# A causal mask in stick-breaking attention: from a TensorE product to a predicated copy and a select

## The chip, the cores and the metric

The kernel runs on one core of one Trainium2 chip. The metric is the device time of one launch in microseconds (us); the median of several executions is compared. Times inside an execution come from a profiled one and count from the start of its span.

## What is computed

The reference is a small decoder trunk of two layers on 1024 positions and a model width of 1024. Layer 0 mixes positions with sliding-window attention, layer 1 with stick-breaking attention; each is followed by a SwiGLU block. The change touches layer 1's mixer alone, whose core is, for each of 16 heads of 64 and each block of 128 queries:

```python
z = jnp.einsum('bqhd,bshd->bhqs', qb, k).astype(jnp.float32) * scale
strict = k_idx < t_idx
log_beta = jax.nn.log_sigmoid(z)
log_one_minus = jnp.where(strict, jax.nn.log_sigmoid(-z), 0.0)
rc = lax.cumsum(log_one_minus, axis=3, reverse=True)
after = jnp.pad(rc[..., 1:], ((0, 0), (0, 0), (0, 0), (0, 1)))
a = jnp.where(strict, jnp.exp(log_beta + after), 0.0)
o = jnp.einsum('bhqs,bshd->bqhd', a.astype(v.dtype), v)
```

The kernel works with the sigmoids themselves: a reversed running product of sigmoid(-z) stands for the exponential of the reversed sum. Where a key is not strictly before its query, the first sigmoid has to count as 1 and the second as 0.

## The kernel before

All of the kernel is one function, `build` (line 65), with nested helpers; `mm` (L107) and `tr` (L115) issue products and transposes, so every one of these has L108 or L116 in the profile, and `sub` (L118) issues a subtraction with L119. Layer 1's mixer works on **eight pairs of heads** (`p` = 0 to 7). For each pair there are three streams of work:

- `proj_gen` (L1026) makes the pair's queries, keys and values from the normalised input: products into the PSUM banks `psd`, then copies to `QK` and `V` with a high part (ScalarE) and a rest (`sub` on DVE). It first loads the pair's weights with `load_b` (L981), whose split into a high part `whl` (ScalarE, L308) and a rest runs on POOL (L309) for two of the three weights of a pair.
- `scores` (L1076) takes one head of the pair (`par`) and two blocks `i` = 2c and 2c+1 of 128 queries against the `L` = 128(i+1) keys up to the end of the block. One or two pieces of at most 512 keys each get two products into a bank `psz` (high and rest of the keys). On the last piece a third product with the bf16 matrices `identb` and `maskb` adds -1e30 where a key is not strictly before the query (L1093). ScalarE then makes `nb` = sigmoid(-z) (L1094) and `bb` = sigmoid(z) (L1095). When the block is whole, DVE runs the reversed running product over `nb` in place (L1101, one scan of L elements) and POOL multiplies `bb` by it (L1103). The result waits in the list `ready`.
- `values` (L1110) runs two steps of the order behind: it transposes `bb` on TensorE into `pst` (L116), splits the transposed tile into `ah` (ScalarE, L1124) and `al` (`sub` on DVE, L119) and multiplies both by `V` into `psa`.

For pairs 0 to 6 `weave` (L1152) interleaves the steps of `scores`, `values` and `proj_gen` of the next pair, for c = 3, 2, 0, 1 with the first head and then the same with the second: the query blocks come as 6, 7, 4, 5, 0, 1, 2, 3, twice in a pair. In these pairs TensorE's order is fixed by hand: `chained` (L99) makes each product follow the one before. The order on the other engines is set by the planner of the framework from the dependencies and the order of the program; each engine then works its queue strictly in that order. The eighth pair has no projection beside it; its scores and values run one after the other, with the split of the output weights (`load_o`, L363 to L369) on DVE and ScalarE between them.

Buffers: `nb` has 3, `bb` 6, `psz` 3 banks, `ah` and `al` 2 each. The constants `identb` and `maskb` are made once at the start (L126 to L135). `up`, a mask of ones above the diagonal that layer 0 uses, is made at L173 to L175 in the same manner as the new `upd`.

Of the kernel before, what the change touches and what calls it, by code (L numbers as in the profile page):

```python
# [9 lines left out]
BF16 = mybir.dt.bfloat16  # L10
I32 = mybir.dt.int32
U32 = mybir.dt.uint32
AF = mybir.ActivationFunctionType
ALU = mybir.AluOpType
# [4 lines left out]
P = 128  # L19
# [7 lines left out]
NEG = -1.0e30  # L27
# [37 lines left out]
def build(tc, x_in, c_in, pos_in, ada_w, ada_b, n1g, n2g, wqkv_a, qn_a, kn_a, sinks, wo_a,  # L65
          wqkv_b, wo_b, w_gate, w_up, w_down, out):
    nc = tc.nc
# [5 lines left out]
    cons = ctx.enter_context(tc.tile_pool(name="cons", bufs=1, side="left"))  # L73
# [8 lines left out]
    def nm(s):  # L82
        uid[0] += 1
        return f"{s}_{uid[0]}"

    def bank(tag, dt=F32):
        return ps.tile([P, 512], dt, tag=tag, name=nm("ps" + tag), bufs=BUFS[tag])
# [11 lines left out]
    def chained(i):  # L99

        if pe["on"] and pe["prev"] is not None:
            tc.add_manual_dep(i.ins, pe["prev"].name,
                              mybir.DependencyInfo(mybir.DependencyClass.NoSync, mybir.DependencyReason.DATA),
                              reason="order")
        pe["prev"] = i.ins if pe["on"] else None

    def mm(o, l, r, start, stop, more=False):  # L107
        chained(nc.tensor.matmul(o, l, r, start=start, stop=stop, skip_group_check=more))  # L108
# [13 lines left out]
    ident = cons.tile([P, P], F32, name="ident")  # L122
    make_identity(nc, ident)
    identr = cons.tile([P, P], F32R, name="identr")
    nc.vector.tensor_copy(identr, ident)
    identb = cons.tile([P, P], BF16, name="identb")  # L126
    nc.vector.tensor_copy(identb, ident)
    ones = cons.tile([P, P], F32, name="ones")
    nc.vector.memset(ones, 1.0)
    mhalf = cons.tile([P, 8], F32, name="mhalf")  # L130
    nc.vector.memset(mhalf, -0.5)

    maskb = cons.tile([P, P], BF16, name="maskb")
    nc.gpsimd.memset(maskb, 0.0)
    nc.gpsimd.affine_select(maskb, maskb, [[-1, P]], ALU.is_gt, NEG, base=0, channel_multiplier=1)  # L135
    negt = cons.tile([P, 1], F32, name="negt")
    nc.vector.memset(negt, NEG)
    up = cons.tile([P, P], U32, name="up")


    cols = cons.tile([P, 32], F32, name="cols")
# [31 lines left out]
    upf = st.tile([P, P], F32, name="upf")  # L173
    nc.gpsimd.affine_select(upf, ones, [[1, P]], ALU.is_gt, 0.0, base=0, channel_multiplier=-1)
    nc.vector.tensor_copy(up, upf)  # L175
    r1 = st.tile([32, P], F32, name="r1")
    r2 = st.tile([96, P], F32, name="r2")
    r3 = st.tile([NB, P], I32, name="r3")
# [897 lines left out]
    def scores(p, par, c, Q, K, kl, V):  # L1076

        bs = []
        for i in (2 * c, 2 * c + 1):
            L = P * (i + 1)  # L1080
            n = max(256, L if L <= 512 else L // 2)
            nb = wb.tile([P, S], F32, tag="nb", name=nm("nb"), bufs=3)
            bb = wb.tile([P, S], F32, tag="bb", name=nm("bb"), bufs=6)
            tq = slice(i * P, i * P + P)
            for s0 in range(0, L, n):
                pz = bank("z")
                o = pz[:, 0:n]
                last = s0 + n >= L
                mm(o, Q[par][:, tq], K[par][:, s0 : s0 + n], True, False)
                mm(o, Q[par][:, tq], kl[par][:, s0 : s0 + n], False, not last)  # L1090
                e = min(n, L - s0)
                if last:
                    mm(pz[:, e - P : e], identb, maskb, False, True)  # L1093
                nc.scalar.activation(nb[:, s0 : s0 + e], pz[:, 0:e], AF.Sigmoid, scale=-1.0)  # L1094
                nc.scalar.activation(bb[:, s0 : s0 + e], pz[:, 0:e], AF.Sigmoid)  # L1095
                if not last:
                    yield
            if i == 2 * c:
                nc.gpsimd.memset(bb[:, L : L + P], 0.0)
            rv = nb[:, 0:L][:, ::-1]  # L1100
            nc.vector.tensor_tensor_scan(rv, rv, ones[:, 0:1].to_broadcast([P, L]), initial=1.0,  # L1101
                                         op0=ALU.mult, op1=ALU.mult)
            nc.gpsimd.tensor_tensor(bb[:, 0 : L - 1], bb[:, 0 : L - 1], nb[:, 1:L], op=ALU.mult)  # L1103
            bs.append(bb)
            if i == 2 * c:
                yield
        ready.append((p, par, c, V, bs))
        yield
# [59 lines left out]
    for p in range(8):  # L1168
        cur = nxt
        if p < 7:  # L1170
            pe["on"], pe["prev"] = True, None
            if p == 6:
                for _ in range(4):
                    xq.tile([P, S], F32R, tag="xq", name=nm("QK"), bufs=NQ)
            gen = proj_gen(p + 1)
            nxt = next(gen)
            for n, (par, c) in enumerate((par, c) for par in range(2) for c in (3, 2, 0, 1)):
                parts = [(scores(p, par, c, *cur), STOPS[c])]
                if len(ready) >= LAG:
                    v = ready.pop(0)  # L1180
                    parts.append((values(*v), 2 * v[2] + 2))
                parts.append((gen, (7, 6, 6, 6)[n % 4]))
                weave(parts)
            drain(gen)
            pe["on"] = False
        else:
            W = wo_tiles(hp_) + wo_tiles(hp_)
            for n, (c, par) in enumerate((c, par) for c in range(4) for par in range(2)):
                drain(scores(p, par, c, *cur))
                while len(ready) > (1 if n < 7 else 0):  # L1190
                    drain(values(*ready.pop(0)))
                load_o(W, wo_b[0], n, row_b, ad, "ad")
# [39 lines left out]
```

## Time and profile before

| quantity | value |
|---|---|
| median of three runs | 2514.96 us (2512.82 to 2516.09) |
| the profiled execution's own time | 2506.01 us |
| its span | 2504.3 us |
| TensorE products busy | 2359.5 us, 94% |
| DVE busy | 1604.8 us, 64% |
| ScalarE (ACT) busy | 1036.6 us, 41% |
| GpSimd (POOL) busy | 646.4 us, 26% |

Stick-breaking attention takes the stretch from about 1199 to 1710 us of the span. In the rows below PE is TensorE, PEld its loading of weights, DVE VectorE, ACT ScalarE and POOL GpSimd. A timeline row gives the start, the duration, the engine, the line, the operation, the tile written and the tiles read, the shapes and how many instructions are merged; what stands in brackets is how long the engine had been idle before and what ended that. Products overlap on TensorE, so that their pace is read from starts and not from durations. A duration includes the time in which an instruction that has started cannot go on.

### The profile page before, as it was taken

How to read it: one execution, taken by the hardware profiler on the slowest of the kernel's cores; microseconds unless marked ns; L12 is line 12 of the kernel's file. 1: busy time of each engine (PE TensorE's matmuls, PEld its weight loads, DVE VectorE, ACT ScalarE, POOL GpSimd, SP SyncE). 2: the span in 40 equal slices, each digit the busy share in tenths (PEclk: the TensorE clock that was granted, in tenths of full speed). 3: DMA queues.
4: the chain of work that ended last, by engine and by line, in shares of the span. 5: the costliest groups of instructions: out<-in, count | busy, mean ns of one | idle time of the engine just before them, and what ended most of it. 6: DMA issues, size and time to landing. Idle time of an engine off the chain costs nothing.

```text
span 2504.3 us, 31440 instructions
## 1 busy us (share of the span) xinstructions
PE 2359.5 (94%) x11404; PEld 1934.1 (77%) x11404; DVE 1604.8 (64%) x2319; ACT 1036.6 (41%) x2029; POOL 646.4 (26%) x671
## 2 busy tenths in 40 slices
PE   6899899799999999999999999988979999999999
PEld 5677677578787878887788888777758888887887
DVE  7679955765767677536677676696375454557553
ACT  4487723423232332104666666573343333323110
POOL 2344512223232300001444444341212322310000
PEclk9799899899999999999999999999989999999999
DMA  8113398143536264203222222127522222227211
GB/s 288 51 50 120 110 228 249 62 130 122 175 120 182 95 238 143 82 9 101 70 58 60 60 56 53 41 80 168 143 76 74 82 93 68 91 86 257 84 51 68
DMA packets 187195, 273.78 MB, mean 109 GB/s; under 512 B 11792, under 2 KB 131744, under 8 KB 187040
## 3 DMA queue, kind: packets, MB, share of 16 engines
q1 hardware_dynamic: 186416, 271.63, 35.2%
q8 instruction: 90, 1.47, 0.2%
q14 instruction: 65, 0.53, 0.1%
q10 hardware_dynamic: 624, 0.14, 0.0%
HBM read 206.72 MB, written 56.62 MB: 105 GB/s over the span
## 4 chain that ended last, share of the span: by engine, by line
PE 70%; DVE 9%; DMA 4%; issue 2%; ACT 2%; POOL 1%; SPq 0%; DVEq 0%; ACTq 0%; POOLq 0%
PE psz L108 24%; PE psd L108 21%; PE pst L108 16%; PE psa L108 5%; DMA ada<-in_ada_w_dram 2%; PE pst L116 2%; DVE nb L1101 2%; DVE acc L268 1%; DVE al L119 1%; DVE lT L119 1%; DVE Wl L309 0%; DMA wr<-in_wo_b_dram 0%; DVE QK L119 0%; DVE sl L631 0%; ACT nb L1094 0%
## 5 line engine op out<-in xcount | busy, mean ns | idle before, releaser
L630 ACT CAST sh<-rg 128x512 fp32r<-128x512 f32 x308 | 191.5, 622 | 565.6 <-PE psz L108 246.1
L631 DVE TENSOR_TENSOR sl<-rg,sh 128x512 fp32r<-128x512 f32 x308 | 244.8, 795 | 94.0 <-ACT sh L630 94.0
L108 PE MATMUL psd<-hth,whl 128*128 128x512 f32 x768 | 304.3, 415 | 0.1
L1103 POOL TENSOR_TENSOR bb<-bb,nb 128x895 f32<-128x895 f32 (+7 forms) x128 | 179.1, 1402 | 248.7 <-DVE nb L1101 159.5
L1101 DVE TENSOR_TENSOR_SCAN nb<-nb,ones 128x896 f32<-128x896 f32 (+7 forms) x128 | 192.4, 1508 | 44.3 <-ACT nb L1094 41.9
L308 ACT CAST dh<-raw 128x1024 fp32r<-128x1024 f32 x88 | 87.9, 1048 | 277.8 <-PE psa L108 174.9
L803 POOL TENSOR_TENSOR rg<-rg,rg 128x512 f32<-128x512 f32 x44 | 58.3, 1324 | 459.8 <-DMA rg<-in_w_up_dram 361.0
L108 PEld LDWEIGHTS psd<-hth,whl 128*128 128x128 f32 x768 | 146.5, 191 | 22.2 <-issue 1.3
L108 PE MATMUL psz<-hT,sh 128*128 128x512 f32 x352 | 139.5, 399 | 19.0 <-ACT hT L684 10.8
L108 PE MATMUL psd<-htl,whl 128*128 128x512 f32 x384 | 152.3, 399 | 1.8 <-DVE htl L119 1.6
L119 DVE TENSOR_TENSOR al<-pst,ah 128x512 fp32r<-128x512 f32 x160 | 108.3, 684 | 62.1 <-ACT ah L1124 59.5
L108 PE MATMUL psz<-lT,sh 128*128 128x512 f32 x352 | 140.0, 398 | 2.7 <-DVE lT L119 2.7
L108 PE MATMUL psz<-hT,sl 128*128 128x512 f32 x352 | 139.0, 395 | 0.0
L108 PE MATMUL psd<-hB,sl 128*128 128x512 f32 x352 | 137.4, 390 | 0.0
L108 PE MATMUL psd<-hB,sh 128*128 128x512 f32 x352 | 137.3, 390 | 0.0
L108 PE MATMUL psd<-lB,sh 128*128 128x512 f32 x352 | 137.0, 389 | 0.0
L268 DVE SCALAR_TENSOR_TENSOR acc<-ada,condT,acc 128x1024 f32<-128x1024 f32 x77 | 111.0, 1441 | 25.5 <-DMA ada<-in_ada_w_dram 24.8
L1094 ACT ACTIVATE nb<-psz 128x448 f32<-128x448 f32 (+3 forms) x192 | 95.3, 496 | 65.6 <-PE psz L108 61.3
L1124 ACT CAST ah<-pst 128x512 fp32r<-128x512 f32 x160 | 94.2, 591 | 54.1 <-PE pst L116 51.8
L309 DVE TENSOR_TENSOR dl<-raw,dh 128x1024 fp32r<-128x1024 f32 x88 | 104.6, 1220 | 9.8 <-ACT dh L308 9.8
L108 PE MATMUL psz<-QK,QK 128*128 128x384 f32 (+4 forms) x384 | 104.7, 356 | 2.5 <-ACT bb L1095 2.4
L108 PE MATMUL psa<-al,V 128*128 128x256 f32 x320 | 88.9, 299 | 17.5 <-DVE al L119 16.7
(325 smaller groups left out, 6336.8 us busy)
## 6 DMA issues: line engine op xcount, KB each, us to landing
ada<-in_ada_w_dram SPq DMA_DIRECT2D x96, 512.0 KB, 4.6
rg<-in_w_gate_dram SPq DMA_DIRECT2D x44, 512.0 KB, 3.6
rg<-in_w_up_dram SPq DMA_DIRECT2D x44, 512.0 KB, 5.7
raw<-hid SPq DMA_DIRECT2D x44, 512.0 KB, 6.6
raw<-in_w_down_dram SPq DMA_DIRECT2D x44, 512.0 KB, 4.4
hid<-f SPq DMA_DIRECT2D x64, 256.0 KB, 2.1
wr<-in_wqkv_b_dram SPq DMA_DIRECT2D x24, 512.0 KB, 4.2
odA<-ob SPq DMA_DIRECT2D x32, 256.0 KB, 2.5
```

The costliest lines, as they stand in the source:

```text
L108: chained(nc.tensor.matmul(o, l, r, start=start, stop=stop, skip_group_check=more))
L119: return nc.vector.tensor_tensor(o, a, h.bitcast(F32), op=ALU.subtract)
L268: i = nc.vector.scalar_tensor_tensor(a, wt, condT[:, j : j + 1], a, op0=ALU.mult, op1=ALU.add)
L308: nc.scalar.copy(h, raw)
L309: (eng or nc.vector).tensor_tensor(l, raw, h.bitcast(F32), op=ALU.subtract)
L630: nc.scalar.copy(hv, src)
L631: nc.vector.tensor_tensor(lv, src, hv.bitcast(F32), op=ALU.subtract)
L803: nc.gpsimd.tensor_tensor(A[1, 0], A[1, 0], A[1, 1], op=ALU.add)
L1094: nc.scalar.activation(nb[:, s0 : s0 + e], pz[:, 0:e], AF.Sigmoid, scale=-1.0)
L1101: nc.vector.tensor_tensor_scan(rv, rv, ones[:, 0:1].to_broadcast([P, L]), initial=1.0, op0=ALU.mult, op1=ALU.mult)
L1103: nc.gpsimd.tensor_tensor(bb[:, 0 : L - 1], bb[:, 0 : L - 1], nb[:, 1:L], op=ALU.mult)
L1124: nc.scalar.copy(ah_, pt)
```

## The change

The mask product is left out, and with it its two constants. The sigmoids of the last 128 keys of a block are masked instead after ScalarE has made them: DVE copies ones over `nb` where a new mask `upd` (made once, on POOL and DVE) is not zero, in front of the scan, and POOL replaces `bb` by zero where the key is not strictly before the query, in front of its multiplication.

```diff
-    identb = cons.tile([P, P], BF16, name="identb")
-    nc.vector.tensor_copy(identb, ident)
...
-    maskb = cons.tile([P, P], BF16, name="maskb")
-    nc.gpsimd.memset(maskb, 0.0)
-    nc.gpsimd.affine_select(maskb, maskb, [[-1, P]], ALU.is_gt, NEG, base=0, channel_multiplier=1)
...
+    upd = cons.tile([P, P], U32, name="upd")
...
+    nc.gpsimd.affine_select(upf, ones, [[1, P]], ALU.is_ge, 0.0, base=0, channel_multiplier=-1)
+    nc.vector.tensor_copy(upd, upf)
...
                 mm(o, Q[par][:, tq], K[par][:, s0 : s0 + n], True, False)
-                mm(o, Q[par][:, tq], kl[par][:, s0 : s0 + n], False, not last)
+                mm(o, Q[par][:, tq], kl[par][:, s0 : s0 + n], False, True)
                 e = min(n, L - s0)
-                if last:
-                    mm(pz[:, e - P : e], identb, maskb, False, True)
                 nc.scalar.activation(nb[:, s0 : s0 + e], pz[:, 0:e], AF.Sigmoid, scale=-1.0)
                 nc.scalar.activation(bb[:, s0 : s0 + e], pz[:, 0:e], AF.Sigmoid)
                 if not last:
                     yield
+            nc.vector.copy_predicated(nb[:, L - P : L], upd, ones)
+            nc.gpsimd.affine_select(bb[:, L - P : L], bb[:, L - P : L], [[-1, P]], ALU.is_gt, 0.0, base=0, channel_multiplier=1)
             if i == 2 * c:
                 nc.gpsimd.memset(bb[:, L : L + P], 0.0)
             rv = nb[:, 0:L][:, ::-1]
```

## Rows read from the trace of the kernel before

**Rows 1.** The page: the chain that ended last, by engine.

```profile
PE 70%; DVE 9%; DMA 4%; issue 2%; ACT 2%; POOL 1%; SPq 0%; DVEq 0%; ACTq 0%; POOLq 0%
```

**Rows 2.** Busy time per stretch: length; PE, PEld, DVE, ACT, POOL; clock; DMA.

```profile
1380.00:1440.00 60.00, 59.40 (x350) 49.39 (x349) 42.75 (x46) 41.50 (x88) 27.98 (x24) 1.00 0.23 62
1660.00:1705.00 45.00, 32.18 (x173) 26.40 (x171) 45.00 (x37) 32.37 (x69) 24.66 (x20) 0.84 0.29 76
```

**Rows 3.** Timeline of TensorE, two score pieces of 448 keys, the second with the mask product.

```profile
1451.72 0.57 PE L108 MATMUL psz<-QK,QK 128*128 128x448 f32 x2
...
1452.36 0.40 PE L108 MATMUL psd<-htl,whl 128*128 128x512 f32 x1
...
1453.96 0.57 PE L108 MATMUL psz<-QK,QK 128*128 128x448 f32 x2
...
1454.73 0.39 PE L108 MATMUL psd<-htl,whl 128*128 128x512 f32 x1
```

**Rows 4.** Timeline of TensorE, the products that wait for `al`, two halves.

```profile
1465.88 0.39 PE L108 MATMUL psa<-al,V 128*128 128x256 f32 x1 [0.48 <-DVE al L119]
...
1498.05 0.38 PE L108 MATMUL psa<-al,V 128*128 128x256 f32 x1
```

**Rows 5.** Timeline of DVE, half of a pair that ends at 1498.

```profile
1487.84 2.02 DVE L1101 TENSOR_TENSOR_SCAN nb<-nb,ones 128x896 f32<-128x896 f32 x1 [0.51 <-ACT nb L1094]
1491.50 2.42 DVE L1101 TENSOR_TENSOR_SCAN nb<-nb,ones 128x1024 f32<-128x1024 f32 x1 [1.64 <-ACT nb L1094]
1493.85 1.38 DVE L119 TENSOR_TENSOR QK<-psd,QK 64x512 fp32r<-64x512 f32 x2
...
1495.87 1.55 DVE L1101 TENSOR_TENSOR_SCAN nb<-nb,ones 128x640 f32<-128x640 f32 x1
```

**Rows 6.** Timeline of ACT, the same half, the last piece of block 7's `bb`.

```profile
1491.30 0.59 ACT L1095 ACTIVATE bb<-psz 128x512 f32<-128x512 f32 x1
```

**Rows 7.** Timeline of POOL, the same half.

```profile
1490.01 1.77 POOL L1103 TENSOR_TENSOR bb<-bb,nb 128x895 f32<-128x895 f32 x1 [3.81 <-ACT ob L1145]
1494.07 2.00 POOL L1103 TENSOR_TENSOR bb<-bb,nb 128x1023 f32<-128x1023 f32 x1 [2.29 <-PE psz L108]
1496.04 3.57 POOL L309 TENSOR_TENSOR whl<-wr,whl 128x1024 fp32r<-128x1024 f32 x1
```

**Rows 8.** One line's instructions on POOL: L309, ns minimum/median/maximum, first and last start.

```profile
L309 POOL TENSOR_TENSOR whl<-wr,whl x14: 2347/2399/3574, 1188.0 to 1586.2; 128x1024 fp32r<-128x1024 f32 x14
```

**Rows 9.** Timeline of DVE, half of a pair that ends at 1466.

```profile
1458.96 2.42 DVE L1101 TENSOR_TENSOR_SCAN nb<-nb,ones 128x1024 f32<-128x1024 f32 x1 [1.64 <-ACT nb L1094]
...
1463.61 1.49 DVE L1101 TENSOR_TENSOR_SCAN nb<-nb,ones 128x640 f32<-128x640 f32 x1
1465.13 0.69 DVE L119 TENSOR_TENSOR al<-pst,ah 128x512 fp32r<-128x512 f32 x1
```

**Rows 10.** Timeline of DVE, last pair.

```profile
1674.29 1.19 DVE L309 TENSOR_TENSOR Wl<-wr,Wh 128x1024 fp32r<-128x1024 f32 x1
1675.40 2.87 DVE L1101 TENSOR_TENSOR_SCAN nb<-nb,ones 128x768 f32<-128x768 f32 x1
...
1688.94 3.56 DVE L1101 TENSOR_TENSOR_SCAN nb<-nb,ones 128x1024 f32<-128x1024 f32 x1
```

**Rows 11.** Timeline of POOL, last pair, and one multiplication from a half before.

```profile
1465.25 1.32 POOL L1103 TENSOR_TENSOR bb<-bb,nb 128x639 f32<-128x639 f32 x1 [1.58 <-DVE nb L1101]
...
1674.51 2.15 POOL L1103 TENSOR_TENSOR bb<-bb,nb 128x639 f32<-128x639 f32 x1 [3.92 <-DVE nb L1101]
...
1688.58 1.77 POOL L1103 TENSOR_TENSOR bb<-bb,nb 128x895 f32<-128x895 f32 x1 [1.49 <-ACT bb L1095]
```

**Rows 12.** Groups by line: DVE's predicated copy of layer 0, DVE's `V` rests.

```profile
L524 DVE COPY_PREDICATED sm<-up,psz 128x256 f32<-128x256 uint32 x56 | 23.1, 439 | 5.2 <-ACT sm L520 4.7
...
L119 DVE TENSOR_TENSOR V<-pst,V 128x256 fp32r<-128x256 f32 x21 | 8.9, 425 | 16.8 <-ACT V L1073 16.7
```

**Rows 13.** One line's instructions: POOL's select for `up`, at the kernel's start.

```profile
L174 POOL TENSOR_SCALAR_AFFINE_SELECT upf<-ones x1: 294/294/294, 1.7 to 1.7; 128x128 f32<-128x128 f32 x1
```

## The prediction

> **What bounds the kernel now.** I read the chain that ended last, then the busy time by stretch, then the timelines of one pair of heads. The chain is TensorE for 70% of the span, DVE for 9% [rows 1], so a product that goes is worth something only where TensorE does not wait, and DVE matters in places. The stretches show two different stages [rows 2]: in the woven pairs 0 to 6 TensorE is busy 59.4 of 60 us at a granted clock of 1.00 (2.4 GHz), in the last pair DVE is busy 45.0 of 45 us, TensorE only 32.2. The timelines of a pair show that even the first stage is not TensorE's alone. Once in each half of a pair (one head's eight blocks) TensorE stops at a product that needs `al`: 0.48 us idle ahead of 1465.88, and a stop too short to be marked ahead of 1498.05 [rows 4]. DVE is what is late: from the scan of block 7 on it has no pause worth the name: scan of 1024, rests of `QK`, an `al`, scan of 640, `al` [rows 5, 9]. So a half has two parts: some 8 us from block 7's scores to that `al`, set by DVE and by POOL beside it, and some 24 us set by TensorE.
>
> **What is removed.** One mask product per block: 16 in a pair, 112 in pairs 0 to 6, 16 in the last. Its price is read by comparing two pieces of 448 keys in the same company, one with and one without it [rows 3]: from the first score product to the second projection product after it, 1451.72 to 1452.36 is 0.64 us, 1453.96 to 1454.73 is 0.77. So 0.13 us each. Of a half's eight, those of blocks 7, 4 and 5 lie ahead of the wait and only lengthen it when they go; five count: 0.65 us a half. ScalarE can start block 7's sigmoids some 0.1 us earlier, which I carry below. In the last pair TensorE waits anyway: nothing.
>
> The Trainium skill, "TensorE: Matmul & The Clock Gate", section "Back-to-back issue gap", gives some 81 ns for a product of 128 columns in a stream with loads. By it 112 products would be an estimated 9.1 us and not 14.6; the trace's 0.13 us is the measurement of this stream and decides.
>
> **What is added.** The copy: 128 columns of f32, which the trace does not show. Layer 0's is 256 wide at 0.439 us [rows 12]. DVE's subtractions of 256 and 512 columns take 0.425 and 0.69 [rows 9, 12], 1.04 ns a column, so half the width is 0.13 less: 0.30 us. Bounds: 0.22 (as wide a share as half of 0.439) and 0.44. The select of 128 x 128 stands in the trace at 0.294 us [rows 13]. The edits at the start exchange a POOL select and a DVE copy for the like, 1.2 ms ahead of this stage: nothing.
>
> Behind the waiting copy stand the scan and then `QK`, `al`, for which TensorE waits. Behind the waiting select stand POOL's multiplication of the same block and the split L309.
>
> **Who may run beside whom.** DVE's scan and POOL's multiplication do not run side by side. At 1688.58 POOL starts 1.77 us of multiplication; the scan of 1024 that starts at 1688.94 takes 3.56 instead of 2.42 [rows 10, 11, 5]. And when two such DVE instructions follow each other, a POOL instruction that is waiting gets in between: at 1674.29 DVE subtracts until 1675.48; POOL's multiplication, started at 1674.51, takes 2.15 instead of 1.32, so it ran from about 1675.3 to 1676.66; the scan queued right behind DVE's subtraction, 1675.40, takes 2.87 and so had to let it pass [rows 10, 11]. In the before a scan is one instruction and POOL waits behind it. The change puts a second one ahead of it, and with it a gap.
>
> The Trainium skill, "SBUF — State Buffer", section "Who interferes with whom", states that DVE with two SBUF inputs and GpSimd reading SBUF exclude each other for a whole instruction. The rows agree for scan and multiplication; no row shows it for the select or the copy. By that rule both take part, each new POOL read included, which speaks against the change. In my sum the select's block has the bounds 0 and 0.29 us; I take 0.29 where it arrives between copy and scan, since the multiplication's row is the nearest.
>
> **A half with the split L309 in it** [rows 5 to 7]. Block 6: copy 0.30, scan to about 1490.1; the select, whose `bb` comes while the scan runs, waits for its end and takes until 1490.4; POOL's multiplication then ends at 1492.2 instead of 1491.78. Block 7: `nb` ready at 1491.3; the copy waits for POOL until 1492.2 and ends at 1492.5; the select, ready since 1491.9, goes next, to 1492.8; the scan (2.42 less 0.13 of waiting) ends at 1495.1 instead of 1493.92. `QK` and an `al`, 1.38 and 0.69 [rows 9], take 2.1: 1497.2. POOL multiplies from 1495.1 to 1497.1 and then has L309, 2.40 us when alone [rows 8]; it took 3.57 because the scan of block 4 was ahead of it. Now the copy arrives when L309 has started, or goes first and lets L309 in before the scan: 1499.5 either way. Copy, select and scan, 0.30 + 0.29 + 1.49, and `al`, 0.69: 1502.3, where TensorE went on at 1498.05 [rows 4]. The wait grows by 4.3 us.
>
> **A half without it** [rows 9]. The scan of block 7 ends 1.2 later, at 1462.6; `al` and `QK` (2.2 from scan to scan) bring 1464.8; POOL has just ended its multiplication, and select and copy, 0.6, make it 1465.3; scan and `al` 1467.5 against 1465.8: some 1.6 us more.
>
> **The sum.** The 3.57 us form of L309 stands in six of the 14 halves (the timeline has it every 64.4 us); in the last of them TensorE soon waits for a weight load anyway, so I count five. 5 x (4.3 - 0.65) = 18.3; 9 x (1.6 - 0.65) = 8.6. In the last pair DVE has no idle time [rows 2], so 16 copies add 16 x 0.30 = 4.8; its selects I leave at nothing, with 16 x 0.29 = 4.7 as the other bound. Together +31.7 us. The rows are of an execution of 2506.0 us, 9 us below the median of 2515.0; the difference is put on the median: **2546 us**.
>
> **Rivals.**
> - *No long block.* L309 comes at another place of POOL's queue (the planner may move it), all else as above: 14 x 0.95 = 13.3, plus 4.8: 2533. For it: POOL's queue gets 16 more instructions a pair. Against: L309 has no tie to the selects and stood between blocks 7 and 4 every time.
> - *Only the copies count.* Select and copy do not exclude the other engine, or do so unnoticed: two copies a half, 0.60, less 0.1 of earlier sigmoids, less 0.65, is -0.15 a half, -2 in all, plus 4.8: 2518. For it: no row shows these two operations in a conflict.
> - *The products come back in full*, on the other side. The mechanism: the planner puts `al` ahead of the copy and the scan of block 4 in DVE's queue, so TensorE no longer meets a late `al`. It decides from the point where DVE is less than 0.65 us later per half. Then 112 x 0.13 = 14.6 less 4.8: 2505. For it: `al` needs only `ah`, and another cost in DVE's queue can turn the planner's order. Against: the same order in all the halves read.
>
> **How the numbers follow.** Forecast 0.41, no long block 0.22, only the copies 0.20, full return 0.17. A measurement of this kernel tells apart about 0.2%, 5 us. Slower by more: 0.41 + 0.22 and a good third of the third case (its copies at 0.44 would add 2.2 in the last pair), 0.70 in all; the rest of that case is within, 0.13; faster 0.17. Upper end: the forecast with the selects in the last pair, 4.7, and with the clock falling to 1.2 GHz after the longer waits. In the last pair, where TensorE waits for `al` again and again, 0.16 of 45 us of clock was lost [rows 2]; five long waits may lose as much, 7, and a longer copy the rest: 2560. Lower end 2508, between the full return and the case of the copies alone; what is left out is most of the full return.
>
> **What would show it.** Right: no `maskb` rows; scans of 1024 at over 3 us from copy to end; L309 at 2.4 us where it had 3.57, with the copy or the scan of block 4 as long as 3 to 4 us beside it; TensorE's waits for `al` at 2 to 5 us a half; DVE still full in the last pair, which is 5 us longer. Wrong: waits for `al` below 1 us in all halves, another order of `al` and the scans, or a last pair no longer than before.

## The result and the profile after

The changed kernel takes **2539.09 us** (median of four runs, 2533.38 to 2541.06) against 2513.89 us before in the same session (2512.01 to 2516.09): a ratio of **1.0096**, with a 95% interval of 1.0081 to 1.0112. It is 25.2 us slower; forecast were 31. The profiled execution has an own time of 2539.56 us and a span of 2537.8 us.

The stage itself is measured best inside the traces, from its first score product to the first product of the SwiGLU block behind it: 637.3 us before (1190.64 to 1827.98), 663.2 us after (1195.94 to 1859.18), **+25.9 us**. Below this is called the stage. It agrees with the 25.2 us of the medians, so the loss lies in it. The spans of the two profiled executions differ by 33.5 us; the other 7.6 lie outside the stage, where nothing of weight was changed, and the stage's start wanders as much between the other kernels (1191.2 to 1199.5 us).

The page's chain by engine of the changed kernel, to be read beside [rows 1]:

```profile
PE 64%; DVE 12%; DMA 6%; issue 3%; ACT 1%; POOL 1%; SPq 0%; DVEq 0%; ACTq 0%; POOLq 0%
```

TensorE's part falls from 70 to 64%, DVE's rises from 9 to 12%. TensorE's waits over the woven pairs (total us, times, longest us), the kernel before, 1199 to 1646 us:

```profile
PE psa L108 <- DVE al L119: 8.1, 8, 3.6
```

The same view of the changed kernel, 1205 to 1673 us:

```profile
PE psa L108 <- DVE al L119: 33.0, 27, 2.8
```

So the new time is TensorE waiting for `al`, about two stops in each of 14 halves of a pair instead of eight in all. (The 3.6 us of the kernel before are a single stop in the second half of pair 5.) The same by stretch, changed kernel, columns as in [rows 2]:

```profile
1380.00:1440.00 60.00, 56.27 (x322) 47.98 (x321) 47.85 (x60) 38.06 (x82) 34.61 (x39) 0.97 0.18 50
1447.81:1455.00 7.19, 5.43 (x31) 4.36 (x28) 7.09 (x6) 5.43 (x12) 4.85 (x4) 1.00 0.34 73
1455.00:1459.00 4.00, 2.37 (x12) 2.11 (x13) 3.97 (x4) 0.65 (x2) 2.78 (x4) 0.87 0.55 164
1456.63:1459.00 2.37, 2.37 (x12) 2.10 (x13) 2.34 (x2) 0.65 (x2) 1.23 (x3) 0.77 0.67 207
1459.00:1461.00 2.00, 2.00 (x9) 1.70 (x8) 1.06 (x2) 0.45 (x2) 1.38 (x1) 0.50 0.00 0
1459.00:1483.82 24.82, 24.82 (x143) 21.50 (x142) 15.17 (x25) 15.98 (x35) 14.20 (x16) 0.95 0.12 38
1483.82:1516.70 32.88, 31.44 (x181) 26.84 (x180) 26.82 (x34) 21.78 (x47) 17.45 (x21) 1.00 0.19 49
1687.20:1732.20 45.00, 30.66 (x150) 23.87 (x148) 45.00 (x47) 30.89 (x66) 31.65 (x32) 0.80 0.26 69
```

TensorE is busy 56.3 of 60 us where it was 59.4, and the granted clock is 0.97 where it was 1.00. DVE is full from 1447.81 to 1459. In the last pair, which lies some 27 us later than before (so its row is 1687.20 to 1732.20, beside 1660 to 1705 of the kernel before), DVE is full as before, 45.00 of 45 us.

**A half with the long split** (L309 before is L307 now). DVE, changed kernel; L1094 is the copy, L1099 the scan; to be read beside [rows 5]:

```profile
1446.81 0.96 DVE L1094 COPY_PREDICATED nb<-upd,ones 128x128 f32<-128x128 uint32 x1 [1.17 <-ACT nb L1090]
1447.81 2.29 DVE L1099 TENSOR_TENSOR_SCAN nb<-nb,ones 128x1024 f32<-128x1024 f32 x1
1450.01 1.39 DVE L119 TENSOR_TENSOR QK<-psd,QK 64x512 fp32r<-64x512 f32 x2
1451.43 0.69 DVE L119 TENSOR_TENSOR al<-pst,ah 128x512 fp32r<-128x512 f32 x1
1452.04 0.37 DVE L1094 COPY_PREDICATED nb<-upd,ones 128x128 f32<-128x128 uint32 x1
1452.44 3.54 DVE L1099 TENSOR_TENSOR_SCAN nb<-nb,ones 128x640 f32<-128x640 f32 x1
1455.91 0.66 DVE L119 TENSOR_TENSOR al<-pst,ah 128x512 fp32r<-128x512 f32 x1
```

POOL beside it, to be read beside [rows 7]; L1095 is the select, L1101 the multiplication:

```profile
1443.67 2.05 POOL L1095 TENSOR_SCALAR_AFFINE_SELECT bb<-bb 128x128 f32<-128x128 f32 x1 [3.22 <-ACT bb L1091]
...
1445.84 1.77 POOL L1101 TENSOR_TENSOR bb<-bb,nb 128x895 f32<-128x895 f32 x1
...
1450.25 2.00 POOL L1101 TENSOR_TENSOR bb<-bb,nb 128x1023 f32<-128x1023 f32 x1 [2.34 <-DVE nb L1099]
1452.20 2.44 POOL L307 TENSOR_TENSOR whl<-wr,whl 128x1024 fp32r<-128x1024 f32 x1
1454.60 1.48 POOL L1095 TENSOR_SCALAR_AFFINE_SELECT bb<-bb 128x128 f32<-128x128 f32 x1
```

ACT beside it, block 7's last `bb`, to be read beside [rows 6]; its start is where `nb` is ready:

```profile
1446.60 0.59 ACT L1091 ACTIVATE bb<-psz 128x512 f32<-128x512 f32 x1
```

The copy of block 7 comes while POOL multiplies block 6 (1445.84 to 1447.61) and takes 0.96 us instead of 0.3. Then the order turns round. Before, the scan of block 4 ran in 1.55 us and L309 waited behind it, 3.57 us [rows 5, 7]. Now the copy of block 4 ends at 1452.41, L307, started at 1452.20, gets in and runs until 1454.64 with nearly its plain time, 2.44 us, and the scan, started at 1452.44, takes 3.54: POOL's multiplication of block 7 at 1450.25 had left the split next in its queue. The select of block 4, 1454.60, ends with that scan. `al`, for which TensorE stands, comes behind that. This long scan of 640 occurs six times in the woven pairs, in the second half of pairs 0 to 5; everywhere else there it takes 1.48 or 1.49.

L309 held DVE up before the change too, but one scan later, behind the `al`. DVE, kernel before, the scan of block 5 in the half of [rows 5]:

```profile
1498.40 2.81 DVE L1101 TENSOR_TENSOR_SCAN nb<-nb,ones 128x768 f32<-128x768 f32 x1 [0.40 <-ACT nb L1094]
```

In the changed kernel that scan takes 1.80 in the halves with the long split. So the split held up a DVE scan by some 1.0 us (2.81 less 1.80) behind which TensorE did not stop; now it holds one up by 2.1 (3.54 less 1.48) that stands ahead of the `al` for which TensorE does.

**A half without it** (a first half of a pair), DVE, to be read beside [rows 9]:

```profile
1482.78 1.00 DVE L1094 COPY_PREDICATED nb<-upd,ones 128x128 f32<-128x128 uint32 x1 [1.13 <-ACT nb L1090]
...
1488.16 0.31 DVE L1094 COPY_PREDICATED nb<-upd,ones 128x128 f32<-128x128 uint32 x1
1488.50 0.69 DVE L119 TENSOR_TENSOR al<-pst,ah 128x512 fp32r<-128x512 f32 x1
1489.11 1.48 DVE L1099 TENSOR_TENSOR_SCAN nb<-nb,ones 128x640 f32<-128x640 f32 x1
1490.51 0.28 DVE L1094 COPY_PREDICATED nb<-upd,ones 128x128 f32<-128x128 uint32 x1
1490.82 2.85 DVE L1099 TENSOR_TENSOR_SCAN nb<-nb,ones 128x768 f32<-128x768 f32 x1
```

Here the planner has put `al` ahead of the scan of block 4. The scan that has to let POOL pass is that of block 5, 2.85 instead of 1.80. TensorE's waits in the two halves, to be read beside [rows 4]:

```profile
1452.17 0.38 PE L108 MATMUL psa<-al,V 128*128 128x256 f32 x1 [0.72 <-DVE al L119]
...
1456.63 0.38 PE L108 MATMUL psa<-al,V 128*128 128x256 f32 x1 [2.67 <-DVE al L119]
...
1489.25 0.39 PE L108 MATMUL psa<-al,V 128*128 128x256 f32 x1 [0.30 <-DVE al L119]
...
1494.31 0.39 PE L108 MATMUL psa<-al,V 128*128 128x256 f32 x1 [1.14 <-DVE al L119]
```

**Where the 25.9 us lie**, from scan of 1024 to scan of 1024, after less before: the five halves with the long split in pairs 0 to 4, 179.70 less 159.45, +20.3; the six first halves of pairs 0 to 5, 195.70 less 192.99, +2.7; the second half of pair 5 and the first of pair 6, 1.3 us shorter each, -2.5; ahead of the first scan +1.4; from the last woven half's scan to the last `psa` product, with the last pair in it, 88.06 to 89.42, +1.4; from there to the SwiGLU block's product +2.7.

### The profile page after: what moved, and what is told of

Read it like the earlier page. It is cut to its first block, busy times and chain, and to the rows that moved or that the text cites. A ratio compares the mean times of both kernels' runs of the same rounds, so it can differ in the third digit from the quotient of the medians.

```text
span 2537.8 us, 31300 instructions
## 1 busy us (share of the span) xinstructions
PE 2362.2 (93%) x11276; PEld 1941.6 (77%) x11276; DVE 1670.2 (66%) x2447; ACT 1035.6 (41%) x2029; POOL 732.6 (29%) x798
## 4 chain that ended last, share of the span: by engine, by line
PE 64%; DVE 12%; DMA 6%; issue 3%; ACT 1%; POOL 1%; SPq 0%; DVEq 0%; ACTq 0%; POOLq 0%
PE psz L108 23%; PE psd L108 19%; PE pst L108 15%; PE psa L108 5%; DMA ada<-in_ada_w_dram 3%; DVE nb L1099 2%; PE pst L116 2%; DVE al L119 1%; DVE acc L266 1%; DVE nb L1094 1%; DVE QK L119 1%; DVE lT L119 1%; DVE sl L629 0%; DVE Wl L307 0%; DMA rg<-odA 0%
## 5 line engine op out<-in xcount | busy, mean ns | idle before, releaser
L629 DVE TENSOR_TENSOR sl<-rg,sh 128x512 fp32r<-128x512 f32 x308 | 237.0, 770 | 95.1 <-ACT sh L628 95.0
L1099 DVE TENSOR_TENSOR_SCAN nb<-nb,ones 128x896 f32<-128x896 f32 (+7 forms) x128 | 197.1, 1541 | 3.3
L1101 POOL TENSOR_TENSOR bb<-bb,nb 128x895 f32<-128x895 f32 (+7 forms) x128 | 164.5, 1286 | 104.7 <-DVE nb L1099 98.2
L1095 POOL TENSOR_SCALAR_AFFINE_SELECT bb<-bb 128x128 f32<-128x128 f32 x128 | 110.7, 865 | 103.1 <-ACT bb L1091 102.8
L266 DVE SCALAR_TENSOR_TENSOR acc<-ada,condT,acc 128x1024 f32<-128x1024 f32 x77 | 114.5, 1487 | 27.5 <-DMA ada<-in_ada_w_dram 26.4
```

The source lines that it names most:

```text
L266: i = nc.vector.scalar_tensor_tensor(a, wt, condT[:, j : j + 1], a, op0=ALU.mult, op1=ALU.add)
L629: nc.vector.tensor_tensor(lv, src, hv.bitcast(F32), op=ALU.subtract)
L1095: nc.gpsimd.affine_select(bb[:, L - P : L], bb[:, L - P : L], [[-1, P]], ALU.is_gt, 0.0, base=0, channel_multiplier=1)
```

## The experiments

Twelve kernels were run, each in five rounds beside the kernel before, in four sessions in which the kernel before took 2512.77, 2511.05, 2509.76 and 2510.06 us. Kernels of different sessions are therefore compared by their ratios, and 0.1% is 2.5 us. The stage is that of one profiled execution.

| kernel | median, us | ratio to before, 95% interval | stage, us |
|---|---|---|---|
| before | 2513.89 | 1 | 637.3 |
| after | 2539.09 | 1.0096 (1.0081 to 1.0112) | 663.2 |
| no mask at all | 2506.51 | 0.9974 (0.9961 to 0.9987) | 631.7 |
| copies alone | 2538.65 | 1.0101 (1.0083 to 1.0119) | 662.0 |
| selects alone | 2512.51 | 0.9993 (0.9981 to 1.0005) | 635.4 |
| a reduction in the copy's place | 2526.71 | 1.0069 (1.0056 to 1.0081) | 656.4 |
| after, split in quarters | 2529.48 | 1.0073 (1.0061 to 1.0085) | 653.6 |
| after, split on DVE | 2527.12 | 1.0055 (1.0040 to 1.0070) | 650.7 |
| no mask, split on DVE | 2500.73 | 0.9963 (0.9950 to 0.9977) | 626.3 |
| mask in the scan | 2506.08 | 0.9978 (0.9968 to 0.9987) | 635.4 |
| the same, select ahead | 2507.32 | 0.9986 (0.9976 to 0.9996) | 634.7 |
| the same, last pair by product | 2506.76 | 0.9984 (0.9974 to 0.9994) | 635.5 |
| mask in the scan, split on DVE | 2500.27 | 0.9958 (0.9945 to 0.9970) | 628.8 |
| before, split on DVE | 2509.80 | 0.9992 (0.9983 to 1.0002) | 635.6 |

The theory: the copy opens a gap in DVE's queue ahead of the scan, POOL's pending instruction goes through it, and `al` is late. The rivals: the loss is the two instructions' own durations; or it is the selects on POOL.

### Neither copies nor selects, and one of them alone

No mask at all leaves the causal mask out of layer 1:

```diff
-            nc.vector.copy_predicated(nb[:, L - P : L], upd, ones)
-            nc.gpsimd.affine_select(bb[:, L - P : L], bb[:, L - P : L], ...)
```

> Neither mask: the changed kernel without its copies and its selects, so the last 128 keys of a block count unmasked; all products, scans and multiplications stay. It prices the removal of the mask products alone. Theory (the loss comes from a POOL instruction that gets in between copy and scan): no copy, no select, so the halves go back to the queue of before; five mask products of 0.13 us a half count, 14 x 0.65 = 9 us below before, about 2505, and TensorE's waits for al as before or 0.3 us longer. Rival (every product counts): 14.6 below, about 2499. Rival (the products cost nothing, since DVE sets the pace): 2512 to 2516.

It is 6.3 us faster than the kernel before in its own session (2512.77), the stage 5.6 us shorter. So the products are worth some 6 us and the whole loss comes from what was added. In a pair, two halves take 63.3 us where they took 64.4.

Copies alone leaves the second sigmoid unmasked, selects alone the first:

```diff
-            nc.gpsimd.affine_select(bb[:, L - P : L], bb[:, L - P : L], ...)
```

> The copies without the selects (the second sigmoid stays unmasked). Theory: the copy alone opens the gap in front of the scan, L307 still gets in ahead of block 4's scan (scan of 640 at over 3 us, L307 at 2.4 instead of 3.6), so most of the loss stays: 2525 to 2533. Rival (the copies' own 0.3 us in DVE's queue): two copies a half are 0.6, given back by the products, 2510 to 2518, no scan of 640 over 2 us. Rival (the selects are the cause): 2505 to 2509.

```diff
-            nc.vector.copy_predicated(nb[:, L - P : L], upd, ones)
```

> The selects without the copies (the first sigmoid stays unmasked). Theory: a scan is again one instruction, so L307 waits behind block 4's scan (3.6 us), the selects wait behind scans and put POOL's multiplications 0.3 us later: 2507 to 2514. Rival (the selects are the cause): 2525 or more. Rival (the copies' own time): as with neither, about 2505.

The copies alone make all of the loss, 2538.65 us, more than was expected of them. DVE of the copies alone shows the pattern of the changed kernel without any select:

```profile
1455.23 0.36 DVE L1094 COPY_PREDICATED nb<-upd,ones 128x128 f32<-128x128 uint32 x1
1455.63 3.55 DVE L1098 TENSOR_TENSOR_SCAN nb<-nb,ones 128x640 f32<-128x640 f32 x1
```

And POOL of the same kernel:

```profile
1455.39 2.44 POOL L307 TENSOR_TENSOR whl<-wr,whl 128x1024 fp32r<-128x1024 f32 x1
```

The selects alone cost the stage 3.7 us over no mask, 2.1 of them in the last pair (87.52 to 89.66). Beside the copies they add 1.2 by the stage and nothing by the ratios (1.0096 and 1.0101); that TensorE already waits for DVE there is the likely reason, which no run separates.

### Is it the copy, or any instruction in its place?

A reduction over the same 128 columns, one SBUF input and no use made of its result, stands where the copy stood. Copies and selects are left out:

```diff
-            nc.vector.copy_predicated(nb[:, L - P : L], upd, ones)
-            nc.gpsimd.affine_select(bb[:, L - P : L], bb[:, L - P : L], ...)
+            mx = cons.tile([P, 1], F32, tag="ss", name=nm("ss"), bufs=3)
+            nc.vector.tensor_reduce(mx, nb[:, L - P : L], axis=AX.X, op=ALU.max)
```

> No copies and no selects (the last 128 keys count unmasked); instead DVE takes the largest of nb's last 128 columns into a spare column ahead of each scan, an instruction with one SBUF input that changes nothing. The queues of DVE and POOL are those of the run with copies alone. Theory of the gap (any DVE instruction ahead of the scan lets L307 start): the scan of 640 again takes 3.5 us in every second half and the time is 2530 to 2540. Rival (the copy itself excludes POOL and is what costs): the reduction runs beside POOL, 2506 to 2516, and the scan of 640 stays at 1.5. Rival (the delay of 0.3 us alone): 2508 to 2515 with scans of 640 at 1.5.

Measured were 2526.71 us, below the expected range, in a session in which the kernel before took 2509.76; the ratio of 1.0069 would be 2531 us beside the 2513.89 of the result. DVE of the kernel with the reduction:

```profile
1448.41 0.28 DVE L1097 TENSOR_REDUCE ss<-nb 128x1 f32<-128x128 f32 x1
1448.79 3.50 DVE L1099 TENSOR_TENSOR_SCAN nb<-nb,ones 128x640 f32<-128x640 f32 x1
```

POOL of the same kernel:

```profile
1448.57 2.38 POOL L307 TENSOR_TENSOR whl<-wr,whl 128x1024 fp32r<-128x1024 f32 x1
```

The gap is there and does the same: L307 starts before the scan and the scan takes 3.50. Of 128 reductions none took over 0.288 us, whatever POOL did. The copies did wait (minimum, median and maximum in ns; the copies and the selects of the changed kernel):

```profile
L1094 DVE COPY_PREDICATED nb<-upd,ones x128: 273/308/1250, 1205.6 to 1728.1; 128x128 f32<-128x128 uint32 x128
...
L1095 POOL TENSOR_SCALAR_AFFINE_SELECT bb<-bb x128: 286/442/2050, 1206.1 to 1728.8; 128x128 f32<-128x128 f32 x128
```

So the loss has two parts. The reduction in that place costs 0.95% over no mask (1.0069 less 0.9974), some 24 us; the copy costs another 0.32% (1.0101 less 1.0069), some 8. By the stage they are 24.7 and 5.6. Nothing of the second part lies in the five halves with the long split, which take 177.2 us with the reduction and 177.5 with the copies alone. The 128 copies of the copies alone take 59.0 us in all and the reductions 35.5, so the copy's own waiting for POOL is the likely cause of the second part; it is not shown by a run of its own.

The Trainium skill, "SBUF — State Buffer", section "Who interferes with whom", states that a DVE instruction with two SBUF inputs contends with a GpSimd instruction that reads SBUF, and that a reduction never does. Both agree here: the copy, with `upd` and `ones` from SBUF, reached 1.25 us, the reduction 0.288.

### The split in quarters, and the split on DVE

If the long split in the gap is the harm, a shorter piece there harms less:

```diff
-            (eng or nc.vector).tensor_tensor(l, raw, h.bitcast(F32), op=ALU.subtract)
...
+                for k in range(0, KT, 2):
+                    eng.tensor_tensor(l[:, k : k + 2], raw[:, k : k + 2], h[:, k : k + 2].bitcast(F32), op=ALU.subtract)
```

> The changed kernel with each L307 split on POOL cut into four instructions of a quarter's length (about 0.7 us each); it computes the same. Theory (one POOL instruction gets in per gap and is served whole): only one quarter lies between copy and scan of block 4, so that scan takes 1.5 + 0.7 = 2.2 us instead of 3.5, TensorE's wait there falls by 1.3 to 2 us and the short clock falls go: 36.0 us halves come to 33.5 to 34.5, in all 2519 to 2528. Rival (POOL's whole work counts, not its grain): the four quarters all go first, scan of 3.5 us or more, 2537 to 2545, since four instructions cost more than one.

DVE of the kernel with quarters, the scan of block 4:

```profile
1444.88 1.90 DVE L1103 TENSOR_TENSOR_SCAN nb<-nb,ones 128x640 f32<-128x640 f32 x1
```

POOL beside it, three quarters of the split merged in one row:

```profile
1444.64 3.35 POOL L311 TENSOR_TENSOR whl<-wr,whl 128x256 fp32r<-128x256 f32 x3
```

One quarter gets in ahead of the scan, the others wait behind it: 1.90 us instead of 3.54. The halves with the split fall from 36.0 to 32.75 us, and the granted clock of a whole pair is 1.00. It is the kernel that shows the long block to be most of the loss in the woven pairs. Its 2529.48 us still lie a little above what was expected: the second half of pair 5 went the other way, 37.24 to 40.88 us, for a reason that the last kernels show.

```diff
-        w = w0 if p == 0 else [load_b(p, j, nc.gpsimd) for j in range(3)]
+        w = w0 if p == 0 else [load_b(p, j) for j in range(3)]
```

> The changed kernel with the rests of the pair's weights (L307) on DVE instead of POOL; it computes the same. Theory: nothing of 2.4 us is left on POOL to get in ahead of block 4's scan, so the 36.0 us halves come down to about the 32.9 of the others and the short clock falls after the long wait go: 2517 to 2524, although DVE gets 14 subtractions of 1.2 us more. Rival (DVE's own load sets the time): slower than the changed kernel, 2540 to 2550. Rival (the selects): as the changed kernel, 2535 to 2541.

With no split on POOL, 2527.12 us, above the 2517 to 2524 of the theory. Every scan of 640 in the woven pairs takes 1.48 us, and still the kernel is slower than the kernel before. DVE with the split on DVE:

```profile
1448.54 1.48 DVE L1099 TENSOR_TENSOR_SCAN nb<-nb,ones 128x640 f32<-128x640 f32 x1
1449.93 0.27 DVE L1094 COPY_PREDICATED nb<-upd,ones 128x128 f32<-128x128 uint32 x1
1450.24 2.85 DVE L1099 TENSOR_TENSOR_SCAN nb<-nb,ones 128x768 f32<-128x768 f32 x1
```

POOL beside it:

```profile
1450.16 1.32 POOL L1101 TENSOR_TENSOR bb<-bb,nb 128x639 f32<-128x639 f32 x1 [2.14 <-DVE nb L1099]
```

Behind the copy something else of POOL's gets in: here block 4's multiplication, which starts at 1450.16 and holds up the scan of block 5 from 1450.24. Whether DVE's extra work is what keeps this kernel slow was asked by the same edit without copies and selects (no mask again):

> Neither copies nor selects, and the rests of the pair's weights on DVE: prices the 14 subtractions on DVE (1.2 us each, 16.8 in all) where nothing else is changed. Theory: they lie mostly in DVE's pauses, 2506 to 2512, so that nearly all of what the changed kernel with this split still loses (2527) is the copies and what gets in ahead of the scans of blocks 7 and 5. Rival (DVE's load): 2518 or more, so that the split explains most of it.

2500.73 us, below the expected range. The split on DVE costs nothing; whether it gains over no mask is not clear by the ratios (0.9963 and 0.9974, with intervals that overlap), by the stage it gains 5.4 us. All of the 0.92% between this kernel and the one with copies and selects, some 23 us (24.3 by the stage), are the mask's.

### A mask with nothing ahead of the scan

The scan computes state = (state x nb) op1 second operand. With max as op1 and a constant tile that is 1 where a key is not strictly before the query and 0 elsewhere, the running product is held at 1 there, and no instruction stands ahead of it:

```diff
+    floor = cons.tile([P, S], F32, tag="acc", name="floor")
+    nc.gpsimd.memset(floor, 0.0)
+    nc.gpsimd.affine_select(floor[:, 0:P], ones, [[-1, P]], ALU.is_ge, 0.0, base=P - 1, channel_multiplier=-1)
...
-            nc.vector.copy_predicated(nb[:, L - P : L], upd, ones)
...
-            nc.vector.tensor_tensor_scan(rv, rv, ones[:, 0:1].to_broadcast([P, L]), initial=1.0,
-                                         op0=ALU.mult, op1=ALU.mult)
+            nc.vector.tensor_tensor_scan(rv, rv, floor[:, 0:L], initial=1.0, op0=ALU.mult, op1=ALU.max)
```

The select moves behind the multiplication, which it then corrects.

> No copy: the mask of the first sigmoid moves into the scan, whose second operation becomes a maximum with a constant that is 1 for masked keys and 0 elsewhere; the select stands behind POOL's multiplication. It computes the same. Theory: a scan with two full SBUF operands takes as long as before (1.5 us for 640) and is one instruction, so L307 waits behind it: as with the selects alone, 2505 to 2513. Rival (the selects cost more behind the multiplication, or a scan with a full second operand is slower): 2520 or more.

2506.08 us, ratio 0.9978: faster than both kernels, and by the ratios some 30 us faster than the changed one. It masks at nearly the price of no mask (0.9974). DVE of this kernel in a half:

```profile
1464.27 2.59 DVE L1097 TENSOR_TENSOR_SCAN nb<-nb,floor 128x1024 f32<-128x1024 f32 x1 [1.48 <-ACT nb L1090]
...
1468.90 1.49 DVE L1097 TENSOR_TENSOR_SCAN nb<-nb,floor 128x640 f32<-128x640 f32 x1
```

Two refinements were tried: the select ahead of the multiplication (a moved line), and the product kept for the last pair, whose TensorE has time to spare.

> As the run before, with the select ahead of POOL's multiplication as in the change. Theory: the copies alone made the loss, so this is within 3 us of the kernel without copies, 2507 to 2514. Rival (copy and select together did it): 2520 or more.

```diff
-                mm(o, Q[par][:, tq], kl[par][:, s0 : s0 + n], False, True)
+                prod = last and p == 7
+                mm(o, Q[par][:, tq], kl[par][:, s0 : s0 + n], False, not prod)
...
+                if prod:
+                    mm(pz[:, e - P : e], identb, maskb, False, True)
```

> The scan with the maximum, the select behind the multiplication in pairs 0 to 6, and in the last pair the mask product of before instead of the select, since there TensorE waits and DVE and POOL exclude each other. It computes the same. Theory: what the selects cost in the last pair (2 us between neither mask and selects alone) goes: 1 to 4 us below the floor scan with selects throughout, 2502 to 2510. Rival (the last pair is indifferent): the same within 1 us.

Both miss a gain: 2507.32 and 2506.76 us, with intervals that overlap that of 0.9978. The place of the select is indifferent, and so are the last pair's selects.

### Both together, and the control

The mask in the scan with the splits of pairs 1 to 7 on DVE, and, as its control, the kernel before with the splits moved alone:

> The scan itself applies the mask (its second operation is max with a constant tile that holds ones where a key is not strictly before the query), so that no instruction stands ahead of it on DVE, the selects stand behind the multiplications on POOL, and the rests of the weights of pairs 1 to 7 are all made on DVE. Theory (the loss came from the copies, and POOL's long split is a cost of its own): both gains add, 2506.1 less some 5 to 6 us of the split, 2499 to 2504, faster than the kernel before and than the kernel after; scans of 640 at 1.5 us everywhere. Rival (DVE is too full to take the splits once the selects delay POOL as well): 2506 to 2514.

> The kernel before, with the rests of all three weights of a pair on DVE and nothing else changed. Theory (the split on POOL costs by itself, whatever the mask does): 2506 to 2510, 4 to 6 us under the kernel before. Rival (the split on DVE gains only where the mask products are gone, since otherwise TensorE has no slack to give): 2511 to 2515.

The first is the best of all, **2500.27 us**, ratio 0.9958 (0.9945 to 0.9970); some 5 us under the mask in the scan alone by the ratios, 6.6 by the stage. The control's 2509.80 us lie in the range of its theory only because the kernel before took 2510.06 there: it gains nothing that can be measured, 0.9992 (0.9983 to 1.0002). So the theory fell. The rival's gain of nothing came, but its reason, that TensorE has no slack to give, is not shown: one half gains with the products in place too, and others lose (below). The largest single gain of the first kernel stands in the second half of pair 5. TensorE's wait there, mask in the scan with the split on POOL:

```profile
1574.70 0.58 PE L108 MATMUL psa<-al,V 128*128 128x256 f32 x1 [4.22 <-DVE al L119]
```

The ten microseconds behind it, same kernel, columns as in [rows 2]:

```profile
1575.00:1585.00 10.00, 10.00 (x52) 9.16 (x52) 4.07 (x8) 3.67 (x9) 1.83 (x5) 0.71 0.04 13
```

The same product with the split on DVE:

```profile
1574.55 0.39 PE L108 MATMUL psa<-al,V 128*128 128x256 f32 x1 [0.32 <-DVE al L119]
```

And the stretch behind it:

```profile
1575.00:1585.00 10.00, 10.00 (x68) 8.88 (x67) 5.65 (x10) 5.26 (x12) 3.74 (x10) 1.00 0.05 15
```

The wait falls from 4.22 us to 0.32, and the granted clock behind it is 1.00 instead of 0.71: 3.9 and 2.9 us, together 6.8; the half takes 33.07 us instead of 39.98.

What DVE waits for there is a load. The first load of the output weights (`load_o`) takes a buffer that the split reads (both come from the pool `ad`, which has two), so it is issued only when the split has ended. The load's wait for POOL (L304 is the split, L360 the load; total us, times, longest us) and DVE's first instruction on the loaded weights, mask in the scan with the split on POOL:

```profile
SPq L360 <- POOL whl L304: 4.1, 1, 4.1
```

```profile
1572.38 1.66 DVE L361 TENSOR_TENSOR wr<-wr,grow 128x1024 f32<-128x1024 f32 x1 [2.43 <-DMA odB<-ob]
```

The split ends at 1568.34, the load is issued at 1568.4 and takes 3.9 us to land. DVE idles for 2.43 us, and the `al` that TensorE needs stands behind L361 in its queue. (The releaser named in the brackets is another transfer; the load landed at the same time.) With the split on DVE the load is issued 5.9 us after the half's first scan instead of 8.6, and DVE does not idle. So this gain is that of a buffer given back earlier, at one place, and not of a lighter POOL in every half. In the kernel with quarters the split ends latest, at 1581.74, 10.2 us after the half's first scan, and TensorE stops 5.02 us.

In the other stretches the five second halves before it lose 0.9 each (31.64 to 32.49), the six first halves 0.2 each (31.64 to 31.85), and some 5 us more are gained ahead of the first scan (2.9) and from the last woven half on (2.0). In the control the half of pair 5 gains 5.2 (38.52 to 33.37) and the five lose 1.0 each (31.89 to 32.93 in the mean); ahead of the first scan it gains 2.4, from the last woven half on 0.1. So with the products in place gain and loss are nearly even.

## Why the prediction was right

Predicted were 2546 us, 31 more than before; it came 25 more, inside the range, by the mechanism of the forecast. (Its own sum of 31.7 would make it 2546.7.) That the total came so near is in part luck: the long block was forecast at 18.3 and came to 20.3, everything else was forecast at 13.4 and came to 5.6, of which 4.1, ahead of the first scan and behind the last product, stood in no term. Step by step:

- **The gap and the long block.** Right. POOL's L307 takes 2.44 us, nearly its plain time, where it took 3.57, the scan of block 4 takes 3.54, and TensorE waits for the `al` behind it. The forecast counted from block 7's ready `nb` 11.0 us to TensorE's going on (1491.3 to 1502.3); it is 10.03 (1446.60 to 1456.63), before 6.75 (1491.3 to 1498.05). The mark is the same in both, the start of ACT on block 7's `bb`. So the wait grows by 3.3 us, not 4.3: copy and select of block 4 were put behind L309 with 0.6 us, and neither stands there, since the copy goes ahead of L307 and the select behind the scan; L307 also ends 0.2 us earlier, and `al` comes closer behind the scan. What makes up for it was in the upper end of the range only, the clock: 0.87 over 4.00 us and 0.95 over 24.82 is 1.8 us lost in a pair. 3.3 less 0.5 for the products (below) plus 1.8 is 4.6; measured are 20.3 / 5 = 4.05 a half, forecast 3.65. So the agreement of this term is that of a wait put too long with a clock left out, and about half a microsecond stays unexplained. The quarters bear the clock out: there the stops of a half fall from 0.72 and 2.67 us to 0.76 and 1.01, 1.6 less, the clock's 1.8 go, and the half becomes 3.3 us shorter.
- **Five halves and not six.** Right. The sixth long block stands in the half in which TensorE waited before, 3.6 us, behind a load of the output weights; L307 now ends earlier, and that half became 1.3 us shorter.
- **The other nine halves**, forecast +0.95 each, 8.6. This step failed: the six at the front grew by 2.7 / 6 = 0.45. The rival's mechanism was half at work: the planner did put `al` ahead of the scan of block 4. The prediction had named another order of `al` and the scans as a sign of being wrong, and in these halves it came. It stopped short of a full return, since the next copy and scan met POOL in the same way, 1.14 us at 1494.31.
- **The copies of the last pair**, forecast +4.8: +1.4. The copies alone show the same, 1.5 over no mask (87.52 to 89.01). DVE is full there in both, and yet the sum of its durations was no price. Part of a full DVE's time is waiting for POOL, and some of it was only moved: the 16 copies take 6.9 us there, and the 16 scans 24.9 instead of 26.3. What absorbed the rest was not tried.
- **The mask products**, 0.13 us each. Too high: two halves of a pair fall by 1.04 us without any mask, 0.52 a half and not 0.65. From the first scan of 1024 to the last in the woven pairs, 13 halves with 104 products, the kernel without the mask is 6.7 us shorter than the kernel before (418.2 for 424.9); where no split stands on POOL, the control's twin without the mask is shorter than the control by the same 6.7 (418.5 for 425.2). That is 0.065 us for a product, so 7.3 us for 112. The Trainium skill, "TensorE: Matmul & The Clock Gate", section "Back-to-back issue gap", gave 9.1 us as an estimate, which is nearer than the 14.6 of the trace's reading and still above what was measured.
- **Who takes part in the exclusion.** Copy and select both do: a copy of 0.3 us takes up to 1.25 beside POOL, a select up to 2.05 beside a scan. The rival in which only the copies' durations count, 2518, fell. No long block, 2533, fell as well: L307 kept its place. In the split on DVE it was brought about, and 2527 came out, still 0.55% slower than before.
- **The selects in the last pair**, at nothing beside the copies: the selects add 0.4 us to the copies there (89.01 to 89.42) and 1.2 in the whole stage.

What stays open: the 2.7 us between the last `psa` product and the SwiGLU block. They stand in all five kernels that have an instruction ahead of the scan (113.8 to 114.5 us) and not in the others (111.0 to 112.7). No run was made for it.

## What to carry to other kernels

An instruction of 0.3 us ahead of a longer one on the same engine is not priced at 0.3 us where two engines exclude each other: ask which instruction of the other engine is waiting at that moment, and count that one's whole duration. Put a mask into an instruction that runs anyway (here the scan's second operation) before adding one to a queue that others wait for. Cut long low-priority instructions of the neighbour engine, or move them, before adding a gap for them to slip through. And before a wait is put down to a busy engine, see whether it is for a buffer which that engine gives back late.

## What the runs showed of the hardware that was not expected

A DVE instruction that itself never waits for POOL (the reduction, 0.288 us at most) still hands POOL its turn: the scan right behind it took 3.50 us instead of 1.49. Most of the price is set by the gap and not by the instruction: 0.95% with the reduction, 1.27% with the copy. And a wait has a price behind it: after the stop of 2.67 us the granted clock was 0.77 until 1459 and then 0.50, which is 1.2 GHz, until 1461; after the stop of 4.22 us it was 0.71 over ten microseconds. The half of the changed kernel with stops of 0.30 and 1.14 us, 1483.82 to 1516.70, stayed at 1.00.
